# Where the 1/rms of a gated group norm is applied: before the branch product, or on its group sums

## The chip, the cores and the metric

The kernel runs on one core of one Trainium2 chip. The metric is device time in microseconds (us) of one launch. Engines: PE (TensorE, matrix products; PEld is its weight load), DVE (VectorE), ACT (ScalarE), POOL (GpSimd, which does not read the matrix accumulators), SP (SyncE, which here only issues DMAs). PSUM is the accumulator memory that PE writes, one bank of it holds 128x512 float32; SBUF is the working memory.

## The reference, cut to what matters

One encoder layer for 256 rows (tokens) of width 1024. The part that the change touches is the end of the SSD branch and the merge:

```python
y_ssd = y_ssd + d_skip[:, None] * xh                       # 256 x 2048
y_ssd = gated_group_rmsnorm(y_ssd, z, ssd_norm)
merged = sigmoid(gate_a) * (y_attn @ w_attn_branch) + sigmoid(gate_b) * (y_ssd @ w_ssd_branch)
x = x + merged @ w_out
x = x + hier_moe(rmsnorm(x))                               # 32 experts, float32 weights

def gated_group_rmsnorm(y, z, g):                          # 4 groups of 512 columns
    yf = y * silu(z)
    yg = yf.reshape(..., 4, 512)
    yg = yg * rsqrt(mean(yg * yg, -1) + EPS)
    return yg.reshape(yf.shape) * g
```

The factor rsqrt(...) is one number for each row and group. The product with w_ssd_branch sums over the columns of all four groups.

## The kernel before, in words

Every float32 operand of the large products is split in two float32r parts, hi and lo (a tile `..._hl`, or yT, mT, hT with a hi and a lo plane), and a product takes three passes: hi·hi, hi·lo, lo·hi. Weights come from memory as `w_raw` (four buffers, SP issues their DMAs in order), ACT casts hi, and DVE or POOL subtracts to get lo. A weight chunk of 512 columns is eight row blocks k of 128 rows, 48 matmuls for its two row tiles t, and its hi and lo go through six buffers that PE must free again. Chunks stand in one list, `wsrc`; `next_w` hands out the next and loads one ahead.

Stages in order: input projections and attention (to about 185 us of the trace), four SSD groups of 512 columns (products xs and z, scans), two chunks A (attention branch product), four chunks S (SSD branch product), the output product o, routing, and the experts. 100 MB of expert weights, tiles `we`, are fetched by `prefetch` calls that stand between the stages; each waits in SP's queue for a buffer that the stage before has freed. From the routing on, PE works through eight sets q of four experts, each with 12 MB of weights.

SSD, group g: `ssd_y(g, q)` makes yg (two 128x256 tiles of columns by rows, so columns lie on partitions), squares it on ACT, and POOL adds the squares into ysum. `ssd_tail(g)` (called later, ahead of others by its priority) sums over the partitions with a matmul by ones (ps_n, L769), forms 1/rms for each row (DVE nv L771, POOL power L100), and, since rows lie on the free dimension of yg, spreads it over the partitions with a product by the identity (ps_r, L775). Then DVE multiplies yg by the gain snorm and ps_r (L781, four times 128x256), ACT casts hi (L783), DVE subtracts lo (L784) into yT[g].

Branch product S, row halves i of w_ssd_branch outside, column halves c inside: `wide_chunk("S", yT[2i:2i+2])` sums two groups into one PSUM tile for each t. DVE multiplies it by (tab_b + 1), where tab holds the tanh of the gates (L832). For i = 0 POOL adds it to the attention part in tab (L834). For i = 1 DVE adds (L836), PE transposes (ps_mT L839), ACT and DVE split into mT, and a `prefetch` follows.

The order on each engine is set by a scheduler with its own timeline, under the priorities in the code; it can move any instruction if others change.

Of the kernel before, what the change touches and what calls it, by code (L numbers as in the profile page):

```python
# [11 lines left out]
F32 = mybir.dt.float32  # L12
# [3 lines left out]
AF = mybir.ActivationFunctionType  # L16
ALU = mybir.AluOpType
# [31 lines left out]
def block_kernel(ctx, tc, xin, idn, ngain, catt, cprep, cssd, cmoe, cwr, wsm, wwide, win, wgu, wdn, out, dbg=None):  # L49
    nc = tc.nc  # L50
    pe, act, dve, pool = nc.tensor, nc.scalar, nc.vector, nc.gpsimd

    cst = ctx.enter_context(tc.tile_pool(name="cst", bufs=1))
# [629 lines left out]
    snorm = C("snorm")  # L683
    yT = [bigt([P, 2, 4, T], F32R, f"yT{g}") for g in range(4)]
# [22 lines left out]
    st_ = {}  # L707
# [30 lines left out]
    def ssd_y(g, q):  # L738
# [3 lines left out]
        st_[g, q, "yg"] = yg  # L742
# [3 lines left out]
        for h2 in range(2):  # L746
# [9 lines left out]
            dve.tensor_tensor(yg[:, h2, :], yg[:, h2, :], zs[:, h2, :], op=ALU.mult)  # L756
        sq = zs_t[g, q]
# [7 lines left out]
    def ssd_tail(g):  # L765
# [4 lines left out]
        r = ssd.tile([P, 2], F32, tag="nv", name="nv")  # L770
        dve.tensor_scalar(r, ps_n, 1.0 / 512, 4 * EPS, op0=ALU.mult, op1=ALU.add)  # L771
        power(r, r, None)
        ps_r = paux.tile([P, T], F32, tag="n", bufs=1, name="ps_r")
        for t in range(2):
            pe.matmul(ps_r[:, t * P:(t + 1) * P], lhsT=r[:, t:t + 1].to_broadcast([P, P]), rhs=ident,  # L775
                      start=True, stop=True)
        for q in range(2):
            yg = st_[g, q, "yg"]
            for b in range(2):
                ct = 4 * g + 2 * q + b  # L780
                dve.scalar_tensor_tensor(yg[:, b, :], yg[:, b, :], snorm[:, ct:ct + 1], ps_r, op0=ALU.mult, op1=ALU.mult)  # L781
            hl = yT[g][:, :, 2 * q:2 * q + 2]
            act.copy(hl[:, 0], yg)  # L783
            dve.tensor_sub(hl[:, 1], yg, hl[:, 0].bitcast(F32))  # L784
# [441 lines left out]
def prep(inp):  # L1226
# [26 lines left out]
    wide += [wa[:, :, o] for o in halves] + [ws[:, 8 * i:8 * i + 8, o] for i in range(2) for o in halves]  # L1253
# [57 lines left out]
```

## Time and profile before

| | |
|---|---|
| median of 3 runs | 583.99 us (583.7 to 587.01) |
| profiled execution, its own time | 585.1 us |
| its span, first to last instruction | 583.3 us |
| PE, DVE, ACT, POOL busy, share of the span | 95%, 57%, 47%, 41% |
| mean granted PE clock | 0.987 of full |
| bytes read | 157.5 MB, mean 272 GB/s |

The profile is one execution: 1.8 us of its time lie outside the span. Busy time of PE counts modelled ends of overlapped matmuls, so what counts is when matmuls start, and the pace between starts.

### The profile page before, as it was taken

The numbers are of one execution on the slowest core, as the hardware profiler recorded it, in microseconds if no ns is written. First come the engines' busy times: TensorE is split into PE (matmuls) and PEld (weight loads), VectorE is DVE, ScalarE is ACT, GpSimd is POOL, SyncE is SP. The second block draws the span as 40 slices with busy tenths as digits, with TensorE's granted clock in tenths as the row PEclk, the third lists the DMA queues.
The fourth block names the chain that finished last, engine by engine and source line by source line (L and its number), as shares of the span: only waits on it lengthen the run. The fifth ranks groups of instructions, "written<-read, shape, count | busy, mean of one in ns | idle before, by whom it ended". The sixth has DMA issues, their size and how long they took to land.

```text
span 583.3 us, 9898 instructions
## 1 busy us (share of the span) xinstructions
PE 552.6 (95%) x3605; PEld 400.6 (69%) x3605; DVE 330.9 (57%) x689; ACT 271.8 (47%) x633; POOL 239.5 (41%) x254
## 2 busy tenths in 40 slices
PE   8999989999999999999999999999998898988976
PEld 5878768798898999898878888964453452433512
DVE  3659975999996778989695657451111121111101
ACT  7567557757987877878764436410000000000001
POOL 4687584775844456656567745210000000000000
PEclk9999999999999999999999999999989997999989
DMA  7755244453435488645568589989999999999993
GB/s 272 250 162 169 103 147 146 144 174 124 128 122 186 149 323 334 217 149 185 208 194 300 177 307 389 405 344 417 419 417 408 420 417 421 409 415 421 420 407 123
DMA packets 35123, 159.27 MB, mean 273 GB/s; under 512 B 4096, under 2 KB 5760, under 8 KB 25856
## 3 DMA queue, kind: packets, MB, share of 16 engines
q1 hardware_dynamic: 33776, 157.30, 71.8%
q10 hardware_dynamic: 1296, 1.30, 0.7%
q8 instruction: 30, 0.49, 0.3%
q14 instruction: 21, 0.17, 0.1%
HBM read 157.54 MB, written 1.05 MB: 272 GB/s over the span
## 4 chain that ended last, share of the span: by engine, by line
PE 69%; DMA 12%; DVE 9%; issue 4%; POOL 3%; ACT 3%; SPq 0%; ACTq 0%; POOLq 0%; DVEq 0%
PE ps_S L294 8%; PE pgu L1037 6%; PE ps_xs L241 6%; PE ps_g L294 6%; DMA we<-wdn 5%; DMA we<-wgu 5%; PE ps_z L241 5%; PE py L1097 4%; PE ps_A L294 4%; PE acc L1112 4%; PE ps_g L1030 4%; PE ps_q L294 3%; PE ps_o L241 2%; PE ps_o L294 2%; PE ps_iq L294 2%
## 5 line engine op out<-in xcount | busy, mean ns | idle before, releaser
L156 POOL TENSOR_TENSOR w_hl<-w_raw,w_hl 128x512 fp32r<-128x512 f32 (+1 forms) x101 | 141.6, 1406 | 81.8 <-ACT w_hl L152 66.5
L152 ACT CAST w_hl<-w_raw 128x512 fp32r<-128x512 f32 (+1 forms) x212 | 125.7, 620 | 46.4 <-PE ps_S L294 18.5
L156 DVE TENSOR_TENSOR w_hl<-w_raw,w_hl 128x512 fp32r<-128x512 f32 (+1 forms) x111 | 100.4, 911 | 38.7 <-ACT w_hl L152 38.1
L1055 POOL TENSOR_TENSOR dc<-Dm,cmr 128x128 f32<-128x128 f32 x16 | 6.1, 401 | 143.5 <-DVE Dm L960 137.4
L1037 PE MATMUL pgu<-we,xg 128*32 128x512 f32 x512 | 60.2, 603 | 3.9 <-DMA we<-wgu 3.9
L241 PE MATMUL ps_z<-hT,w_hl 128*128 128x256 f32 x384 | 51.7, 286 | 0.0
L241 PE MATMUL ps_xs<-hT,w_hl 128*128 128x256 f32 x384 | 50.7, 285 | 0.0
L241 PEld LDWEIGHTS ps_z<-hT,w_hl 128*128 128x128 f32 x384 | 47.8, 190 | 2.0 <-issue 2.0
L241 PEld LDWEIGHTS ps_xs<-hT,w_hl 128*128 128x128 f32 x384 | 47.6, 191 | 2.1 <-issue 2.1
L294 PE MATMUL ps_g<-w_hl,gT 128*128 128x512 f32 x192 | 48.1, 399 | 0.0
L294 PE MATMUL ps_S<-w_hl,yT 128*128 128x512 f32 x192 | 44.6, 391 | 0.0
L1033 DVE TENSOR_TENSOR xg<-ps_g,cmoe 128x512 f32<-128x512 f32 (+2 forms) x18 | 11.3, 631 | 57.4 <-PE ps_g L1030 57.4
L1030 PEld LDWEIGHTS ps_g<-Dm,x_sb 128*128 128x128 f32 x256 | 31.0, 191 | 14.9 <-issue 9.7
L294 PEld LDWEIGHTS ps_g<-w_hl,gT 128*128 128x128 f32 x192 | 34.9, 188 | 9.3 <-DVE w_hl L156 1.0
L294 PEld LDWEIGHTS ps_S<-w_hl,yT 128*128 128x128 f32 x192 | 35.8, 188 | 7.4
L1037 PEld LDWEIGHTS pgu<-we,xg 128*32 128x32 f32 x512 | 15.1, 110 | 37.1 <-issue 26.1
L1097 PE MATMUL py<-we,aTt 128*32 128x512 f32 (+1 forms) x272 | 35.8, 616 | 3.8 <-DVE aTt L1083 2.1
L1108 ACT COPY y<-py 128x512 f32<-128x512 f32 (+1 forms) x9 | 4.8, 539 | 66.9 <-PE py L1097 66.9
L1075 DVE SCALAR_TENSOR_TENSOR ac<-th,pgu 128x256 f32<-128x256 f32 x8 | 3.4, 421 | 57.5 <-ACT th L1073 57.5
L1112 PE MATMUL acc<-y,dcT 128*128 128x512 f32 (+1 forms) x68 | 32.6, 606 | 0.9 <-DVE y L1110 0.8
L1030 PE MATMUL ps_g<-Dm,x_sb 128*128 128x128 f32 x256 | 33.4, 280 | 0.0
L1073 ACT ACTIVATE th<-pgu,rs 128x256 f32<-128x256 f32 x8 | 3.8, 474 | 55.1 <-PE pgu L1037 55.1
(296 smaller groups left out, 968.9 us busy)
## 6 DMA issues: line engine op xcount, KB each, us to landing
we<-wgu SPq DMA_DIRECT2D x55, 1024.0 KB, 13.8
w_raw<-wwide SPq DMA_DIRECT2D x60, 512.0 KB, 3.9
w_raw<-win SPq DMA_DIRECT2D x44, 512.0 KB, 3.9
we<-wdn SPq DMA_DIRECT2D x17, 1024.0 KB, 17.4
we<-wdn SPq DMA_DIRECT2D x28, 512.0 KB, 12.0
we<-wgu SPq DMA_DIRECT2D x18, 512.0 KB, 10.2
x_sb<-xin SPq DMA_DIRECT2D x2, 512.0 KB, 4.4
we<-wdn SPq DMA_DIRECT2D x4, 256.0 KB, 11.5
```

Of the source, the lines that this page charges most:

```text
L152: return act.copy(self.hl[i][:, 0], self.raw[i])
L156: return eng.tensor_sub(hl[:, 1], self.raw[i], hl[:, 0].bitcast(F32))
L241: pe.matmul(ps, lhsT=lhs[k][:, a], rhs=rhs[k][:, b], start=j == 0 and k == 0 and i == 0, stop=j == len(regions) - 1 and k == KD - 1 and i ...
L294: pe.matmul(ps[t], lhsT=lhs[t][k][:, a], rhs=w[k][:, b], start=k == 0 and i == 0, stop=k == KD - 1 and i == 2)
L1030: pe.matmul(ps[:, kk, :], lhsT=x1[:, t, (k + kk) * P:(k + kk + 1) * P], rhs=Dm[:, t].rearrange("p e j -> p (e j)"), start=t == 0, stop=t == 1)
L1033: dve.tensor_tensor(xg[:, ks, :], ps, fgain[:, ks].unsqueeze(2).to_broadcast([P, n, P]), op=ALU.mult)
L1037: i = pe.matmul(pgu[32 * e:32 * e + 32, :], lhsT=xg[:, k, 32 * e:32 * e + 32], rhs=wg[k][e], start=k == 0, stop=k == KD - 1, tile_position ...
L1055: pool.tensor_tensor(dc[:, t], Dm[:, t], cmr[:, t, 4 * q:4 * q + 4].unsqueeze(2).to_broadcast([P, 4, NSLOT]), op=ALU.mult)
L1073: act.activation(th, pgu[:, 0:256], AF.Tanh, scale=rs)
L1097: i_py = pe.matmul(py[32 * e:32 * e + 32, :], lhsT=aTt[:, f, 32 * e:32 * e + 32], rhs=wd[2 * n + f][e][:, c], start=f == 0, stop=f == 1, t ...
L1108: act.copy(y, py)
L1112: pe.matmul(acc[t][n][:, c], lhsT=dcT[:, t * P:(t + 1) * P], rhs=y, start=False, stop=q == 7 and c.stop == 512)
```

## The change

The gain snorm stays with yg, and 1/rms is left out of yT. `ssd_y` now splits yg at once: ACT writes hi = yg * snorm, DVE writes lo = yg * snorm - hi, each in two pieces of 128x256. `ssd_tail` keeps only ps_n and the power, into one tile rg for all groups; ps_r, the four multiplications, the casts and the subtractions of the tail are gone. In the S stage each group has a PSUM sum of its own, rows on partitions, so 1/rms is a scalar for each partition: the first group's sum goes through ACT with that scale into a tile m, the next two are multiplied by rg and added on DVE, and after two groups more the gate is applied. tab_b gets its + 1 once, on ACT. Column halves are now outside, row halves inside, and the list of weights follows (`ws[...] for o in halves for i in range(2)`).

```diff
+    rg = cst.tile([P, 4, 2], F32, name="rg")
...
+        hl = yT[g][:, :, 2 * q:2 * q + 2]
+        for b in range(2):
+            ct = 4 * g + 2 * q + b
+            act.activation(hl[:, 0, b], yg[:, b], AF.Copy, scale=snorm[:, ct:ct + 1])
+            dve.scalar_tensor_tensor(hl[:, 1, b], yg[:, b], snorm[:, ct:ct + 1], hl[:, 0, b].bitcast(F32),
+                                     op0=ALU.mult, op1=ALU.subtract)
...
-        r = ssd.tile([P, 2], F32, tag="nv", name="nv")
+        r = rg[:, g]
         dve.tensor_scalar(r, ps_n, 1.0 / 512, 4 * EPS, op0=ALU.mult, op1=ALU.add)
         power(r, r, None)
-        ps_r = paux.tile([P, T], F32, tag="n", bufs=1, name="ps_r")
-        for t in range(2):
-            pe.matmul(ps_r[:, t * P:(t + 1) * P], lhsT=r[:, t:t + 1].to_broadcast([P, P]), rhs=ident, ...)
-        for q in range(2):
-            yg = st_[g, q, "yg"]
-            for b in range(2):
-                ct = 4 * g + 2 * q + b
-                dve.scalar_tensor_tensor(yg[:, b, :], yg[:, b, :], snorm[:, ct:ct + 1], ps_r, ...)
-            hl = yT[g][:, :, 2 * q:2 * q + 2]
-            act.copy(hl[:, 0], yg)
-            dve.tensor_sub(hl[:, 1], yg, hl[:, 0].bitcast(F32))
...
-    for i in range(2):
-        for c in range(2):
-            ps = wide_chunk("S", yT[2 * i:2 * i + 2], LAG)
+    for c in range(2):
+        for t in range(2):
+            act.activation(tab[t, c][:, 1], tab[t, c][:, 1], AF.Copy, bias=1.0)
+        U = [mo2.tile([P, 512], F32, tag="y", name="mg") for _ in range(2)]
+        for i in range(2):
...
+                    if kk % 4 == 0:
+                        pss[t, g] = (pacc.tile([P, 512], F32, tag=f"acc{t}1", name="ps_S") if g
+                                     else pmm.tile([P, 512], F32, tag="mm", name="ps_S"))
...
+            for g, t in ((0, 0), (0, 1), (1, 0), (1, 1)):
                 ta, tb = tab[t, c][:, 0], tab[t, c][:, 1]
-                m = mo2.tile([P, 512], F32, tag="y", name="mg")
-                dve.scalar_tensor_tensor(m, tb, 1.0, ps[t], op0=ALU.add, op1=ALU.mult)
-                if i == 0:
-                    pool.tensor_add(ta, m, ta)
+                ps, m, r1 = pss[t, g], U[t], rg[:, 2 * i + g, t:t + 1]
+                if 2 * i + g == 0:
+                    act.activation(m, ps, AF.Copy, scale=r1)
+                elif 2 * i + g < 3:
+                    dve.scalar_tensor_tensor(m, ps, r1, m, op0=ALU.mult, op1=ALU.add)
+                    if i:
+                        dve.tensor_mul(m, m, tb)
+                        pool.tensor_add(ta, m, ta)
+                if 2 * i + g < 3:
                     continue
+                dve.scalar_tensor_tensor(m, ps, r1, tb, op0=ALU.mult, op1=ALU.mult)
                 dve.tensor_add(m, m, ta)
```

PE, around the tail of group 0, before (ps_z is the product for z of group 2, py the scan products, ps_b a spread of decays):

```order
L241 MATMUL ps_z_3087<-hT_209,w_hl 128x256 x10
L749 MATMUL py<-e_2902,xdt_2895 64x256
L775 MATMUL ps_r<-ident,nv 128x128 x2
L749 MATMUL py<-e_2902,xdt_2895 64x256
L752 MATMUL py<-e_2902,xdt_2895 64x128 x2
L749 MATMUL py<-e_2903,xdt_2895 64x256
L729 MATMUL ps_b<-acsT,iir 128x256
L749 MATMUL py<-e_2903,xdt_2895 64x256
L752 MATMUL py<-e_2903,xdt_2895 64x128 x2
L241 MATMUL ps_z_3087<-hT_209,w_hl 128x256 x14
```

The same place now:

```order
L241 MATMUL ps_z_3088<-hT_209,w_hl 128x256 x13
L749 MATMUL py<-e_2911,xdt_2904 64x256 x2
L241 MATMUL ps_z_3088<-hT_209,w_hl 128x256 x7
L752 MATMUL py<-e_2911,xdt_2904 64x128 x2
L730 MATMUL ps_b<-acsT,iir 128x256
L241 MATMUL ps_z_3088<-hT_209,w_hl 128x256
L749 MATMUL py<-e_2912,xdt_2904 64x256 x2
L752 MATMUL py<-e_2912,xdt_2904 64x128 x2
L241 MATMUL ps_z_3088<-hT_209,w_hl 128x256 x3
```

ps_r is gone, and matmuls of the z product now stand between the scan products.

DVE, end of the first pass over S, before (`trs` is a small table for the routing):

```order
L832 SCALAR_TENSOR_TENSOR mg<-tab,ps_S 128x512 x2
L156 TENSOR_TENSOR w_hl<-w_raw,w_hl 128x512 x4
L832 SCALAR_TENSOR_TENSOR mg<-tab,ps_S 128x512 x2
L836 TENSOR_TENSOR mg<-mg,tab 128x512 x2
L156 TENSOR_TENSOR w_hl<-w_raw,w_hl 128x512 x2
```

The end of the first column half now:

```order
L156 TENSOR_TENSOR w_hl<-w_raw,w_hl 128x512 x3
L848 SCALAR_TENSOR_TENSOR mg<-ps_S,rg,mg 128x512 x2
L850 TENSOR_TENSOR mg<-mg,tab 128x512 x2
L156 TENSOR_TENSOR w_hl<-w_raw,w_hl 128x512
L854 SCALAR_TENSOR_TENSOR mg<-ps_S,rg,tab 128x512
L855 TENSOR_TENSOR mg<-mg,tab 128x512
L854 SCALAR_TENSOR_TENSOR mg<-ps_S,rg,tab 128x512
L156 TENSOR_TENSOR w_hl<-w_raw,w_hl 128x512
L855 TENSOR_TENSOR mg<-mg,tab 128x512
L156 TENSOR_TENSOR w_hl<-w_raw,w_hl 128x512 x2
```

Eight instructions on sums stand where four stood, and splits of the next weights stand behind and between them.

SP, the stretch with the weights of S and the expert tiles we_11 and we_0, before:

```order
L270 DMA we_10_3942<-wdn 128x2048
L141 DMA w_raw<-wwide 128x1024 x10
L270 DMA we_11_4261<-wdn 128x2048
L270 DMA we_0_4263<-wgu 128x2048
L141 DMA w_raw<-wwide 128x1024 x4
```

And now:

```order
L270 DMA we_10_3939<-wdn 128x2048
L141 DMA w_raw<-wwide 128x1024 x7
L270 DMA we_11_4168<-wdn 128x2048
L270 DMA we_0_4170<-wgu 128x2048
L141 DMA w_raw<-wwide 128x1024 x8
```

The two expert tiles now go out one weight chunk earlier, ahead of the last chunk of S.

## Rows read from the trace of the kernel before

**Rows 1.** The page: busy time by engine.

```profile
PE 552.6 (95%) x3605; PEld 400.6 (69%) x3605; DVE 330.9 (57%) x689; ACT 271.8 (47%) x633; POOL 239.5 (41%) x254
```

**Rows 2.** The chain that ended last, near its end: start us, us, what.

```profile
541.82 19.88 DMA we<-wgu
561.74 1.94 PE pgu L1037 x8
```

**Rows 3.** Windows: PE, PEld, DVE, ACT, POOL busy, PE clock, DMA share, GB/s.

```profile
185.00:308.00 123.00, 122.84 (x915) 108.28 (x912) 106.14 (x190) 92.75 (x204) 72.46 (x61) 1.00 0.63 221
...
308.00:353.00 45.00, 45.00 (x208) 37.41 (x207) 26.20 (x38) 20.58 (x36) 28.13 (x23) 1.00 0.78 263
...
388.00:390.00 2.00, 2.00 (x17) 1.04 (x17) 0.75 (x3) 0.00 (x0) 0.76 (x2) 1.00 0.32 127
...
400.00:560.00 160.00, 143.25 (x1006) 64.09 (x1004) 25.88 (x60) 9.55 (x20) 4.55 (x12) 0.97 1.02 417
```

**Rows 4.** SP's waits from 376 to 410: us in total, times, longest.

```profile
SPq L270 <- PE pgu L1037: 13.3, 7, 8.2
```

**Rows 5.** Timeline of PE around the ps_r of each group: start us, us.

```profile
212.07 0.65 PE L749 MATMUL py<-e,xdt 128*64 128x256 f32 x4
...
212.88 1.33 PE L241 MATMUL ps_z<-hT,w_hl 128*128 128x256 f32 x9
...
235.70 0.65 PE L749 MATMUL py<-e,xdt 128*64 128x256 f32 x2
...
238.82 1.34 PE L241 MATMUL ps_z<-hT,w_hl 128*128 128x256 f32 x9
...
261.59 0.61 PE L775 MATMUL ps_r<-ident,nv 128*128 128x128 f32 x4
262.04 0.27 PE L716 MATMUL ps_x<-ident,xs 128*128 128x128 f32 x1
...
292.23 0.65 PE L749 MATMUL py<-e,xdt 128*64 128x256 f32 x4
...
293.82 0.38 PE L729 MATMUL ps_b<-acsT,iir 128*128 128x256 f32 x1
...
321.78 0.61 PE L775 MATMUL ps_r<-ident,nv 128*128 128x128 f32 x4
322.14 25.90 PE L294 MATMUL ps_S<-w_hl,yT 128*128 128x512 f32 x113
```

**Rows 6.** Groups of instructions, 184 to 360 us: count, busy us, mean ns, idle before.

```profile
L606 DVE SCALAR_TENSOR_TENSOR xs<-xs,acc 128x256 f32<-128x256 f32 x12 | 7.8, 666 | 0.0
L784 DVE TENSOR_TENSOR yT<-yg,yT 128x512 fp32r<-128x512 f32 x8 | 7.8, 974 | 0.3 <-ACT yT L783 0.3
...
L834 POOL TENSOR_TENSOR tab<-mg,tab 128x512 f32<-128x512 f32 x4 | 5.6, 1400 | 1.8 <-DVE mg L832 1.8
...
L832 DVE SCALAR_TENSOR_TENSOR mg<-tab,ps_S 128x512 f32<-128x512 f32 x8 | 5.3, 678 | 1.7 <-PE ps_S L294 1.7
L783 ACT CAST yT<-yg 128x512 fp32r<-128x512 f32 x8 | 5.1, 637 | 0.9 <-DVE yg L781 0.9
...
L605 ACT ACTIVATE xs<-acc 128x256 f32<-128x256 f32 x12 | 4.8, 416 | 3.1 <-DVE acc L603 3.1
L836 DVE TENSOR_TENSOR mg<-mg,tab 128x512 f32<-128x512 f32 x4 | 3.9, 1008 | 0.0
```

**Rows 7.** The tile yg: ns min/median/max of its DVE instructions.

```profile
L756 DVE TENSOR_TENSOR yg<-yg,zs x16: 410/465/1308, 213.6 to 309.8; 128x256 f32<-128x256 f32 x16
L781 DVE SCALAR_TENSOR_TENSOR yg<-yg,cssd,ps_r x16: 462/475/480, 237.0 to 323.6; 128x256 f32<-128x256 f32 x16
```

**Rows 8.** Groups 307 to 360 us: weight splits on DVE and ACT in the S stage.

```profile
L152 ACT CAST w_hl<-w_raw 128x512 fp32r<-128x512 f32 x35 | 21.5, 623 | 25.5 <-PE ps_S L294 18.5 <-DMA w_raw<-wwide 3.2 <-issue 1.9
L156 DVE TENSOR_TENSOR w_hl<-w_raw,w_hl 128x512 fp32r<-128x512 f32 x18 | 15.9, 889 | 15.6 <-ACT w_hl L152 15.5
```

**Rows 9.** SP's timeline: issue of the expert tiles in S.

```profile
337.84 1.24 SPq L270 DMA_DIRECT2D we<-wdn  x1
```

More of the change, by code (lines that the diff above doesn't have):

```diff
@@ L824, in block_kernel @@
     pacc = ctx.enter_context(tc.tile_pool(name="pacc", bufs=1, space=PSUM, reuse_waits="tile"))
-    for i in range(2):
-        for c in range(2):
-            ps = wide_chunk("S", yT[2 * i:2 * i + 2], LAG)
-            for t in range(2):
-                ta, tb = tab[t, c][:, 0], tab[t, c][:, 1]
-                m = mo2.tile([P, 512], F32, tag="y", name="mg")
-                dve.scalar_tensor_tensor(m, tb, 1.0, ps[t], op0=ALU.add, op1=ALU.mult)
-                if i == 0:
-                    pool.tensor_add(ta, m, ta)
+    for c in range(2):
[3 more added lines that the diff above has]
+        for i in range(2):
+            w = pairs(next_w(), slice(0, 512))
+            src = pairs(yT[2 * i:2 * i + 2], slice(0, T))
+            pss = {}
+            for k in range(KD + LAG):
+                for t in range(2):
+                    kk = k - LAG * t
+                    if not 0 <= kk < KD:
+                        continue
+                    g = kk // 4
+                    if kk % 4 == 0:
+                        pss[t, g] = (pacc.tile([P, 512], F32, tag=f"acc{t}1", name="ps_S") if g
+                                     else pmm.tile([P, 512], F32, tag="mm", name="ps_S"))
+                    for a, b in PASSES:
+                        pe.matmul(pss[t, g], lhsT=src[kk][:, a, t * P:(t + 1) * P], rhs=w[kk][:, b],
+                                  start=kk % 4 == 0 and (a, b) == PASSES[0], stop=kk % 4 == 3 and (a, b) == PASSES[2])
+            for g, t in ((0, 0), (0, 1), (1, 0), (1, 1)):
+                ta, tb = tab[t, c][:, 0], tab[t, c][:, 1]
+                ps, m, r1 = pss[t, g], U[t], rg[:, 2 * i + g, t:t + 1]
[7 more added lines that the diff above has]
+                if 2 * i + g < 3:
                     continue
+                dve.scalar_tensor_tensor(m, ps, r1, tb, op0=ALU.mult, op1=ALU.mult)
                 dve.tensor_add(m, m, ta)
@@ L1252, in prep @@
     halves = [slice(0, 512), slice(512, 1024)]
-    wide += [wa[:, :, o] for o in halves] + [ws[:, 8 * i:8 * i + 8, o] for i in range(2) for o in halves]
+    wide += [wa[:, :, o] for o in halves] + [ws[:, 8 * i:8 * i + 8, o] for o in halves for i in range(2)]
     wwide = np.stack(wide + [wo[:, :, 0:512]])
```

4 lines of the change are left out of this document (removed).

## The prediction

> **What bounds the kernel now.** I read the busy shares first, then the chain from its end, then the windows, and last PE's timeline, stage by stage. PE is busy 95% of the span and DVE 57% [rows 1], but the average hides two programs. The chain ends in expert weights: a transfer of 19.88 us until 561.7, with PE's last expert products right behind it [rows 2], and from 400 to 560 the DMA engines are full, at 417 GB/s [rows 3]. So the end is set by when that stream begins to flow without a break. The window 388 to 390 answers that: there DMA falls to a share of 0.32 [rows 3], because every free buffer is filled and SP waits, 8.2 us at the longest, for PE's first expert products (pgu) to free one [rows 4]. From then on the stream never stops. The end is therefore the time at which PE reaches pgu, plus a constant. PE gets there through stages in which it starts matmuls almost without gaps: 113 matmuls of S in 25.9 us, 0.229 us each [rows 5]. What counts for this change is whatever makes PE arrive at about 388 earlier or later, one for one. DVE, ACT and POOL count only where PE waits for them.
>
> **The change, part by part.**
>
> *ps_r leaves PE.* An undisturbed py block (half of a head group) takes 0.81 us, 212.07 to 212.88. In group 0 the two py blocks around ps_r, with one small ps_b, take 3.12 us (235.70 to 238.82), where two blocks alone take 1.62: 1.50. Group 1: 0.45 (261.59 to 262.04). Group 2: a py block with ps_r inside takes 1.59 (292.23 to 293.82) less 0.81: 0.78. Group 3: 0.36 (321.78 to 322.14) [all rows 5]. Sum 3.1; I take **-3.0** for the ps_b in the first. The bounds are 4 x 0.36 = 1.4, if the rest of those waits has other causes and stays, and 3.1.
>
> *DVE and ACT in the SSD stage.* Removed: 16 multiplications at 0.475 [rows 7] and 8 subtractions at 0.974 [rows 6], 15.4 us of DVE; and 8 casts at 0.637, 5.1 of ACT. Added: 16 lo pieces of 128x256 with two SBUF inputs. The nearest row is L606, the same operation and shape, 0.666: 10.7 us. And 16 hi pieces on ACT, nearest L605, 0.416: 6.7 us [rows 6]. DVE gains 4.7 us, ACT loses 1.6 over 140 us. DVE is busy 106 of 123 us here, ACT 93 [rows 3], so neither sets PE's pace by volume; zero on PE, with the waits already counted at ps_r. If that cover were gone, it would show as DVE gain, so zero is the cautious side.
>
> The new lo pieces read two SBUF tensors; the multiplications that they replace read PSUM for one. The rows tell these apart: with PSUM 462 to 480 ns, with two SBUF inputs 410 at best and 1308 at worst [rows 7]. The Trainium skill (SBUF — State Buffer, Who interferes with whom) says why, and it speaks against this change: a DVE instruction with two SBUF inputs contends with a GpSimd one that reads SBUF, and the later of the two blocks fully. The trace agrees with the spread; by the rule taken at its worst the change would come out slower, the third rival below.
>
> *+ 1 on tab.* Four ACT instructions of 128x512, nearest L783, 0.637: 2.5 us, which the order puts at about 100 to 130 us, in the attention. Something waits behind each on ACT (casts of weights, the move of qT). ACT is not that stage's limit; I put **+0.3** on PE, between 0 and 2.5.
>
> *The S stage.* PE's 192 matmuls stay. The sums of one group instead of two: 16 instead of 8. Four go to ACT (0.637 each by L783, 2.5 us), 12 to DVE at 0.678 where 8 were: +2.7; four multiplications by tab_b, nearest L836, 1.008: +4.0; the additions on POOL and DVE stay four and four [rows 6]. DVE goes from 26.2 busy in 45 us [rows 3] to some 29, since the group 3 tail (four L781 and two L784, 3.8 us) leaves the window. Volume is no problem: ACT's casts of weights wait 18.5 us for PE here [rows 8], so splits run ahead as far as six buffers allow. The order is the problem. At the end of each column half DVE has to take the last sums before the next splits: 0.678 + 1.008 + 0.678 + a split of 0.889 [rows 6, 8] = 3.3 us after the last group of the first row tile, and an addition of 1.400 on POOL has to be done before. PE has work that needs no new split for about 11 matmuls there, 2.5 us at 0.229. So each of the two ends costs 0 to 0.8 us, or up to 2.2 if the POOL addition is late by its whole length. The ps_n of group 3 now stands after 24 matmuls of S, where 36 stood, and behind ACT's two new hi pieces. I take **+1.3** for all these, between 0 and 5.
>
> *Expert prefetch.* Two tiles of 1 MB went out at 337.84 and after [rows 9], when the third S chunk's code was through; now they follow the second chunk, some 11 us earlier (48 x 0.229). From 308 to 353 DMA has 22% free, 9.9 us [rows 3], and 2 MB take 5.0 us at 417 GB/s. It fits. It lengthens the dry spell at 388 and brings nothing there, since PE's arrival still decides; it does make sure that the stream does not come after PE. Zero. SP passes four more weight loads behind these two tiles; the four raw buffers are waited for anyway.
>
> **Sum:** -3.0 + 0.3 + 1.3 = -1.4 us on the profiled execution: span 583.3 to 581.9, its own time 585.1 to 583.7. The median of the runs is 1.1 below that execution: 583.99 - 1.4 = **582.6 us**.
>
> **Rivals.**
>
> 1. *S takes its sums for free.* The order may place the splits well enough that PE never waits in S, and yg, free of the tail, may remove other small waits in the SSD stage. For it: ACT and DVE were idle about half the S stage [rows 8]. Against: the splits stand behind the sums in DVE's order. Then -3.0 to -4.5: 579.5 to 581.
>
> 2. *DVE's in-order queue makes PE wait at the ends of the halves* (the other side). Place: the sums of groups 2 and 3, with POOL's additions among weight splits of 1.4 us each. It decides as soon as the chain there is over 2.5 us by more than the 3.0 that ps_r gives back, spread over two ends and the start of S, that is from 1.5 us at each end on. At 2.2 for each end and 2 for ps_n of group 3 and the first order change of chunks: +6.4 - 3.0 = +3.4, 587.4; at the threshold 584. For it: eight DVE instructions in the place of four. Against: 45 us with 26 busy.
>
> 3. *The shared reads of DVE and POOL.* If each of the 14 lo pieces before 308 us were blocked for a whole POOL operation (0.410 + 1.400 = 1.8 us), DVE's 106.1 would become 106.1 - 5.7 - 5.8 + 25.3 = 119.9 of 123; with the idle of before (17 us) kept, the stage would last 137: +14 - 3 = +11, 595. The mean of L606 at 0.666, in the same mix of POOL work, speaks against all of it.
>
> 4. *Nothing arrives at the end.* If the stream had been ready later than PE, PE's gain would be lost and the time stay at 584.0. Against it is the dry window at 388.
>
> **How the numbers follow.** Forecast (582.6, its own range 581 to 584) 0.55; rival 1 0.17; rival 2 0.18; rival 3 0.02; rival 4 0.08. Of each of the tails about a tenth is left out: the range reaches from rival 1's far end, 579.5, to inside rival 2, 586.5. One per cent, about what a measurement of this kernel can tell from no change, is 5.8 us. Faster by that needs more than twice all that ps_r costs: 0.06. Slower by that needs rival 3, or rival 2 well past its price: 0.06. The rest, 0.88, is within.
>
> **What would show it.** Right: two py blocks near 236 with their ends about 1.5 us sooner; S beginning 2 to 3 us earlier than 307.6; 192 matmuls of S within 45 to 47 us; the dry DMA window now 3 us or more long and ending one to two us earlier than 391; then the same 417 GB/s. Rival 2 would show PE idle, or PE's weight load waiting for w_hl from DVE or POOL, just after the last matmul of a half. Rival 3 would show lo pieces of over 1 us in the mean. I am wrong altogether if the stretch before 185 us, where only the order moves, shifts by more than 1.5 us, or if the stream breaks off again after 392.

## The result and the profile after

| | before | after |
|---|---|---|
| median of 17 runs each | 583.99 us | 587.69 us (585.76 to 590.53) |
| ratio after to before, 95% interval | | 1.0067 [1.0055, 1.0079] |
| profiled execution, its own time | 585.1 us | 587.59 us |
| its span | 583.3 us | 585.7 us |

Slower by 3.7 us, where 1.4 us less was forecast. The page's busy line of the changed kernel and the end of its chain answer to [rows 1, 2]:

```profile
PE 550.4 (94%) x3589; PEld 398.1 (68%) x3589; DVE 342.5 (58%) x689; ACT 276.8 (47%) x649; POOL 246.0 (42%) x254
...
544.53 19.89 DMA we<-wgu
564.47 1.93 PE pgu L1056 x8
```

PE has 16 matmuls less (ps_r) and is busy 2.2 us less, yet the last expert products start 2.7 us later (561.74 before). DVE, which was to have 4.7 us less work in SSD and 6.7 more in S, is 11.6 busier. The windows (columns as in [rows 3]):

```profile
185.00:308.00 123.00, 122.32 (x903) 107.03 (x899) 109.44 (x186) 94.59 (x211) 73.17 (x62) 1.00 0.62 218
308.00:353.00 45.00, 44.13 (x203) 36.18 (x200) 34.05 (x44) 22.94 (x42) 30.55 (x23) 1.00 0.80 273
...
390.00:394.00 4.00, 4.00 (x33) 2.08 (x33) 0.74 (x3) 0.00 (x0) 0.76 (x2) 1.00 0.64 230
400.00:560.00 160.00, 142.65 (x1008) 63.90 (x1000) 26.45 (x61) 10.03 (x21) 4.56 (x12) 0.98 1.02 417
```

The stream of experts is the same (417 GB/s), and there is a dry spell ahead of it as before, only 2 us later. So 2.0 of the 2.7 us lie ahead of 390 (first expert product 388.26 before, 390.25 after); the other 0.7 are taken up below the table. PE's timeline of the changed kernel at the borders of its stages (start us, us, what, and in brackets PE's wait and who ended it; L840 is S, L294 and L241 are the 512- and the 256-column chunks of o, L886 the warm-up products of the routing):

```profile
151.61 1.96 PE L241 MATMUL ps_xs<-hT,w_hl 128*128 128x256 f32 x15
...
308.12 4.84 PE L840 MATMUL ps_S<-w_hl,yT 128*128 128x512 f32 x20
313.84 0.61 PE L776 MATMUL ps_n<-ones,ysum 128*128 128x1 f32 x4 [0.87 <-POOL ysum L768]
314.31 21.36 PE L840 MATMUL ps_S<-w_hl,yT 128*128 128x512 f32 x93
...
353.45 4.70 PE L294 MATMUL ps_o<-w_hl,mT 128*128 128x512 f32 x20
...
359.35 0.60 PE L858 MATMUL ps_mT<-ident,mg 128*128 128x128 f32 x4
360.73 0.39 PE L241 MATMUL ps_o<-w_hl,mT 128*128 128x256 f32 x1 [0.78 <-ACT w_hl L152]
...
384.49 2.54 PE L886 MATMUL ps_w<-on 128*128 128x512 bf16 x11
...
390.25 1.06 PE L1056 MATMUL pgu<-we,xg 128*32 128x512 f32 x8
```

The same borders before (L769 is ps_n):

```profile
315.83 0.50 PE L769 MATMUL ps_n<-ones,ysum 128*128 128x1 f32 x4
...
353.07 5.83 PE L294 MATMUL ps_o<-w_hl,mT 128*128 128x512 f32 x24
...
382.51 2.54 PE L867 MATMUL ps_w<-on 128*128 128x512 bf16 x11
...
388.26 1.07 PE L1037 MATMUL pgu<-we,xg 128*32 128x512 f32 x8
```

Two gaps are new: ahead of ps_n of group 3 and at the start of o. To compare kernels, PE's way is cut by these starts: from the first x product (which came at 150.5 to 152.2 us in all profiles, the same kernel included, so it is the zero here) to the first o matmul, from there to the warm-up products, to the first expert product, and to the last one. Before's first entry, for example, is 353.07 - 152.15. In the three kernels marked * one matmul of o stands among the last of S; there the border is the start of the other o matmuls less 0.23.

| kernel | SSD and S | o | warm-up | to last pgu | ratio to before, 95% |
|---|---|---|---|---|---|
| before | 200.92 | 29.44 | 5.75 | 173.48 | |
| after | 201.84 | 31.04 | 5.76 | 174.22 | 1.0067 [1.0055, 1.0079] |
| order_alone * | 200.92 | 32.37 | 5.75 | 174.10 | 1.0079 [1.0047, 1.0110] |
| order_alone_mT_first * | 200.92 | 29.23 | 5.75 | 174.04 | 1.0016 [1.0001, 1.0031] |
| order_prefetch_late * | 200.93 | 31.28 | 8.20 | 173.87 | 1.0036 [1.0018, 1.0055] |
| before_prefetch_early | 200.92 | 29.87 | 5.79 | 173.40 | 1.0067 [1.0043, 1.0090] |
| prefetch_late | 201.90 | 32.34 | 5.75 | 174.55 | 1.0100 [1.0077, 1.0124] |
| sums_in_pmm | 200.89 | 31.28 | 5.75 | 173.23 | 1.0030 [1.0012, 1.0047] |
| pmm_weights_first | 200.84 | 31.06 | 5.77 | 174.55 | 1.0037 [1.0023, 1.0052] |
| pmm_mT_first | 200.87 | 29.35 | 5.75 | 174.81 | 1.0004 [0.9989, 1.0019] |
| pmm_mT_zs_first | 199.98 | 29.32 | 5.75 | 174.99 | 0.9994 [0.9979, 1.0009] |
| old_order_pmm | 200.83 | 32.03 | 8.02 | 173.00 | 1.0054 [1.0034, 1.0074] |
| ps_r_twice | 204.13 | 29.21 | 5.75 | 174.34 | 1.0078 [1.0062, 1.0094] |

In after, 0.9 us are lost up to o and 1.6 in o. A second profile of the changed kernel (after_look, below) gave 201.86, 30.80, 5.75 and 173.90: the first three repeat within 0.3 us. They need not: three profiles of before_prefetch_early (experiment 3) took 200.92, 202.07 and 200.94 up to o, so a difference of 1 us in one profile counts here only where the wait that makes it is seen in the trace. The last column scatters by 2 us with no relation to the edits, and is largest where PE comes early. It is read as the stream's own scatter, not as a cause; no experiment tested that.

### The profile page after: what moved, and what is told of

Its sections match the earlier page's. It is cut to its first block, busy times and chain, and to the rows that moved or that the text cites. A ratio compares the mean times of both kernels' runs of the same rounds, so it can differ in the third digit from the quotient of the medians.

```text
span 585.7 us, 9882 instructions
## 1 busy us (share of the span) xinstructions
PE 550.4 (94%) x3589; PEld 398.1 (68%) x3589; DVE 342.5 (58%) x689; ACT 276.8 (47%) x649; POOL 246.0 (42%) x254
## 4 chain that ended last, share of the span: by engine, by line
PE 55%; DVE 18%; DMA 13%; ACT 6%; issue 5%; POOL 3%; ACTq 0%; SPq 0%; DVEq 0%; POOLq 0%
PE pgu L1056 6%; PE ps_S L840 6%; DMA we<-wdn 5%; DMA we<-wgu 5%; DVE w_hl L156 4%; PE py L1116 4%; PE ps_xs L241 4%; PE ps_g L1049 4%; PE acc L1131 4%; PE ps_z L241 3%; PE ps_q L294 2%; PE ps_g L294 2%; PE ps_o L241 2%; DVE acc L603 2%; PE ps_iq L294 2%
## 5 line engine op out<-in xcount | busy, mean ns | idle before, releaser
L156 POOL TENSOR_TENSOR w_hl<-w_raw,w_hl 128x512 fp32r<-128x512 f32 (+1 forms) x101 | 145.3, 1445 | 78.4 <-ACT w_hl L152 63.1
L156 DVE TENSOR_TENSOR w_hl<-w_raw,w_hl 128x512 fp32r<-128x512 f32 (+1 forms) x111 | 106.0, 963 | 25.4 <-ACT w_hl L152 24.9
L241 PE MATMUL ps_z<-hT,w_hl 128*128 128x256 f32 x384 | 51.9, 286 | 0.0
L241 PE MATMUL ps_xs<-hT,w_hl 128*128 128x256 f32 x384 | 50.6, 285 | 0.6 <-DVE zs L703 0.6
L241 PEld LDWEIGHTS ps_z<-hT,w_hl 128*128 128x128 f32 x384 | 47.8, 190 | 2.6 <-issue 2.2
L241 PEld LDWEIGHTS ps_xs<-hT,w_hl 128*128 128x128 f32 x384 | 47.5, 191 | 2.9 <-issue 2.1
L294 PE MATMUL ps_g<-w_hl,gT 128*128 128x512 f32 x192 | 47.8, 398 | 0.0
L840 PE MATMUL ps_S<-w_hl,yT 128*128 128x512 f32 x192 | 45.1, 392 | 0.0
L1049 PEld LDWEIGHTS ps_g<-Dm,x_sb 128*128 128x128 f32 x256 | 31.3, 191 | 15.5 <-issue 11.1
L294 PEld LDWEIGHTS ps_g<-w_hl,gT 128*128 128x128 f32 x192 | 35.1, 188 | 8.8 <-DVE ss_q L333 0.8
L840 PEld LDWEIGHTS ps_S<-w_hl,yT 128*128 128x128 f32 x192 | 35.7, 188 | 7.8 <-DVE w_hl L156 0.4
L1131 PE MATMUL acc<-y,dcT 128*128 128x512 f32 (+1 forms) x68 | 30.7, 576 | 0.1
```

The source lines that it names most:

```text
L156: return eng.tensor_sub(hl[:, 1], self.raw[i], hl[:, 0].bitcast(F32))
L241: pe.matmul(ps, lhsT=lhs[k][:, a], rhs=rhs[k][:, b], start=j == 0 and k == 0 and i == 0, stop=j == len(regions) - 1 and k == KD - 1 and i ...
L294: pe.matmul(ps[t], lhsT=lhs[t][k][:, a], rhs=w[k][:, b], start=k == 0 and i == 0, stop=k == KD - 1 and i == 2)
L840: pe.matmul(pss[t, g], lhsT=src[kk][:, a, t * P:(t + 1) * P], rhs=w[kk][:, b], start=kk % 4 == 0 and (a, b) == PASSES[0], stop=kk % 4 == 3 ...
L1049: pe.matmul(ps[:, kk, :], lhsT=x1[:, t, (k + kk) * P:(k + kk + 1) * P], rhs=Dm[:, t].rearrange("p e j -> p (e j)"), start=t == 0, stop=t == 1)
L1131: pe.matmul(acc[t][n][:, c], lhsT=dcT[:, t * P:(t + 1) * P], rhs=y, start=False, stop=q == 7 and c.stop == 512)
```

## The experiments

**1. The order of the halves alone.** The kernel before, with

```diff
-    for i in range(2):
-        for c in range(2):
+    for c in range(2):
+        for i in range(2):
             ps = wide_chunk("S", yT[2 * i:2 * i + 2], LAG)
```

and the list of weights to match; the prefetch after `i == 1` so comes after the second weight chunk.

> The kernel before with one thing changed: column halves outside and row halves inside in S, with the weight list and the expert prefetch behind them; sums, 1/rms and splits as before. Theory: the changed kernel loses in four places, at ps_n of group 3 (about 1.1 us of PE waiting, from the PSUM of the group sums), in the o stage (1.6 us, from the order that an early prefetch gives), in the stream after 398 us (about 0.5), and in the SSD stage, where nothing was gained. Only the middle two can be here: 584.5 to 586. Rival A, the order of the halves is the whole loss: 587 to 588. Rival B, the order of the halves costs nothing: 583.5 to 584.5.

588.65 us, 4.0 more than the kernel before in the same runs: rival A, and beyond it. The SSD and S stages are those of before to 0.01 us, and o takes 2.9 us more. ACT's and PE's timelines at the start of o show how:

```profile
359.64 1.14 ACT L152 CAST w_hl<-w_raw 128x512 fp32r<-128x512 f32 x2 [2.48 <-DMA w_raw<-win]
360.69 0.64 ACT L844 CAST mT<-ps_mT 128x256 fp32r<-128x256 f32 x2
```

```profile
357.65 1.03 PE L839 MATMUL ps_mT<-ident,mg 128*128 128x128 f32 x8
360.31 0.38 PE L241 MATMUL ps_o<-w_hl,mT 128*128 128x256 f32 x1 [1.63 <-ACT w_hl L152]
361.04 1.21 PE L241 MATMUL ps_o<-w_hl,mT 128*128 128x256 f32 x8 [0.34 <-DVE w_hl L156]
```

ACT's next instruction is the cast of the first 256-column weights of o, and they land at 359.6. The casts of mT, whose whole input is there from 358.7 on, stand behind it. PE's next instruction is a matmul on the same weights, so both engines wait for one DMA while 24 matmuls of the 512-column chunk could run (experiment 2 has them at 358.71). In the kernel before, ACT had the first casts of mT ahead:

```profile
359.38 0.81 ACT L844 CAST mT<-ps_mT 128x256 fp32r<-128x256 f32 x2 [1.14 <-PE ps_mT L839]
360.53 1.14 ACT L152 CAST w_hl<-w_raw 128x512 fp32r<-128x512 f32 x2 [0.34 <-DMA w_raw<-win]
```

**2. The casts of mT ahead.** order_alone, with the splits of that chunk (number 36) behind the last cast of mT, which `last_mT` keeps:

```diff
+                if n == 36:
+                    st.enter_context(tc.issue_after(last_mT[0].ins))
                 wready[n].split(KSP_FEW if n in FEW else KSP)
```

> order_alone (kernel before with column halves outside) with one thing more: the splits of the first 256-column chunk of o are issued behind the last cast of mT, so ACT cannot stand waiting for those weights (2.48 us at 357.2 to 359.6 in order_alone) while the casts of mT queue behind it. Theory: the order on ACT and PE at the start of the o stage is what order_alone loses: PE's wait of 1.63 and 0.34 us goes, o comes back from 32.4 to 30 us or less, the time from 588.6 to 585.5 to 586.5. Rival: the weights are late for PE in any order, and the wait moves to the place where the 256-column matmuls now begin: 587.5 to 589.

585.10 us, 0.9 more than before in the same runs, o in 29.23. The same places:

```profile
358.29 1.68 ACT L847 CAST mT<-ps_mT 128x256 fp32r<-128x256 f32 x4 [1.12 <-PE ps_mT L842]
359.86 1.14 ACT L152 CAST w_hl<-w_raw 128x512 fp32r<-128x512 f32 x2
```

```profile
357.65 1.03 PE L842 MATMUL ps_mT<-ident,mg 128*128 128x128 f32 x8
358.71 5.72 PE L297 MATMUL ps_o<-w_hl,mT 128*128 128x512 f32 x24
```

The theory holds: the sequence of a few instructions on ACT and PE was worth 3 us, and the work is the same.

**3. What puts the order wrong: halves or prefetch?** Three kernels move the prefetch of the first two expert tiles alone, `if i: prefetch(...)` to `if c: prefetch(...)` with the loops as they stand: in order_alone back to the third chunk (order_prefetch_late), in the kernel before on to the second (before_prefetch_early), in the changed kernel back (prefetch_late).

> order_alone with the first two expert tiles of S issued after the third weight chunk again, so that only the order of the halves is left. Theory: the early tiles let the scheduler count on the o weights too soon; with the tiles late, ACT's casts of mT stand ahead again and half or more of the 4 us comes back: 584.5 to 586. Rival: it is the order of the halves that makes the o stage late, whatever the tiles do: 587.5 to 589.

587.10 us: half of the loss comes back, and neither side is right alone. At o's start the waits are nearly gone, but o still takes 31.3 us; the profile has the granted clock at half from 382 on, so its last part and its 8.20 us of warm-up (below, the last section) are no measure of the edit.

> The kernel before with one thing changed: the first two expert tiles of S are issued after the second weight chunk, as in the changed kernel, with the order of the halves as before. The prediction put this at zero. Theory: it is not zero, since it moves the o weights and the casts in the scheduler's order: 585.5 to 588. Rival, the prediction: 583.5 to 584.8.

588.62 us, so the prediction's zero for the prefetch is wrong, but the profile shows 29.87 in o and no more. Its own time, 585.5, was the fastest of seven, so two more profiles were taken:

> before_prefetch_early once more, for a second profile. Its profile showed 0.5 us more than the kernel before up to the first expert product, and the fastest of its times, 585.5; its median was 588.6. Theory: in most executions the granted clock falls to half near 382 us, in the routing, as in the profiles of old_order_pmm and order_prefetch_late, where the stretch from the last warm-up products to the first expert product took 8.0 and 8.2 us in place of 5.75: with 588 us the profile shows that. Rival: the stream of expert weights is what is longer by 3 us, with the clock full until 424.

> The same again, for a third profile: a half clock near 382 us with 587 us and more, none with 586 us and less (theory); a longer stream (rival).

586.55 and 584.16 us. Up to o they took 202.07 and 200.94, then 29.87 in o and 5.79 in the warm-up both; to the last pgu 173.75 and 173.30. The clock was full until 424 us or later in both, and the stream was not longer. The rival is not seen; the theory speaks of executions of 587 us and more, and neither was one, so it stays untested. In the first, PE waited for late weights inside S (0.35 and 0.20 us above its pace near 342 and 344 the longest, POOL's split named once), 1.1 us in all. Why most runs took 588 stays open. The mean granted clock on record is 0.982 to 0.983 in the five runs from 587.66 us on and 0.985 and 0.988 in the two below, so the longer ones had more half clock somewhere; a mean does not say where.

> The changed kernel with the first two expert tiles of S issued after the code of the third weight chunk again, as before the change, in place of the second. Theory: PE's order in the o stage then takes the wide product before the first matmul of the 256-column one, the wait of 0.78 us for its weights at 360 us goes, and about 1 to 1.6 us come back: 586.1 to 586.7. Rival: the o stage is late because the last sums of S are late (the chain of DVE behind the last matmul), so the wait only gets another name: 587.4 to 588.

590.31 us: the wait took another name, and grew. PE's timeline:

```profile
359.75 0.63 PE L858 MATMUL ps_mT<-ident,mg 128*128 128x128 f32 x4 [0.91 <-DVE mg L855]
...
361.68 1.20 PE L294 MATMUL ps_o<-w_hl,mT 128*128 128x512 f32 x4 [0.84 <-DVE mT L864]
```

The 512-column chunk now comes first on PE, as expected, but ACT's two casts of the o weights still stand ahead of three casts of mT, and DVE's last sums end 1.2 us later than in after. So late tiles alone do not cure the changed kernel: the order around the start of o decides, and each edit deals it anew. What early tiles cost by themselves stays open with the 588.62 above.

**4. Where the group sums lie.** The changed kernel, its first S chunk with all four sums in the three buffers of the wide products:

```diff
-                        pss[t, g] = (pacc.tile([P, 512], F32, tag=f"acc{t}1", name="ps_S") if g
+                        pss[t, g] = (pacc.tile([P, 512], F32, tag=f"acc{t}1", name="ps_S") if g and c + i
                                      else pmm.tile([P, 512], F32, tag="mm", name="ps_S"))
```

> The changed kernel with all four group sums of the first S chunk in the three PSUM buffers that wide products use, not two of them in the memory that the SSD stage's small PSUM tiles held. Theory: group 1's sums need no longer wait for that memory, so ps_n of group 3 can stand behind 31 matmuls of S in place of 24, and PE's gap at 312.6 to 313.8 us closes: -1.1 us, 586.6. Rival: the squares of group 3 are what is late, PE waits there for them anyway or for a PSUM buffer instead: 587.4 to 588.

586.38 us, SSD and S 0.95 us shorter. PE's timeline, to be read against 313.84 above:

```profile
308.36 6.44 PE L840 MATMUL ps_S<-w_hl,yT 128*128 128x512 f32 x27
314.63 0.51 PE L776 MATMUL ps_n<-ones,ysum 128*128 128x1 f32 x4
315.00 3.35 PE L840 MATMUL ps_S<-w_hl,yT 128*128 128x512 f32 x13
```

The pool `pacc` lies over the five PSUM banks of the SSD stage's small tiles, ps_n among them, and is opened when that stage closes. With group 1's sums in it, no matmul of group 1 came ahead of ps_n, whose squares were not ready: in the changed kernel ACT did the last hi piece ahead of the square, and POOL the sum after that, until 313.8 (ACT, then POOL):

```profile
310.74 0.51 ACT L761 ACTIVATE yT<-yg,cssd 128x256 fp32r<-128x256 f32 x1 [1.93 <-DVE yg L756]
311.16 0.61 ACT L765 ACTIVATE zs<-yg 128x512 f32<-128x512 f32 x1
```

```profile
312.73 1.06 POOL L768 TENSOR_TENSOR ysum<-ysum,zs 128x256 f32<-128x256 f32 x1
```

Before, ps_n stood behind 36 matmuls of S, at 315.83, and waited for nothing. The Trainium skill (Perfetto Trace Analysis, Matmul Optimizations) asks to use all eight PSUM banks. Here the kernel with fewer banks in this place was the faster one, 1.0030 against 1.0067: the banks were not free, they still belonged to a stage whose last product was late. (The wait is for that place in PE's order and not for the bank's reader: the first S matmul behind ps_n starts at 314.31, and DVE reads ps_n at 314.49.)

**5. The o weights ahead of the expert tiles.** sums_in_pmm with `prefetch(PF1[2] + PF1[3])` behind the call that loads the first 256-column weights.

> sums_in_pmm with the first 256-column weights of o issued ahead of the last two expert tiles of the S stage, in place of behind them. Theory: those weights stand behind 2 MB of expert tiles on the DMA engines and so land at 359.5 us; ahead of them they land some 3 to 5 us sooner, ACT does not wait (3.03 us in sums_in_pmm) and PE's wait of 1.02 us at 360 goes: 585 to 585.5 against 586.4, and no loss in the stream, since the tiles are only waited for after 390. Rival: what ends the wait is mT, which the last sums set, and it stays: 586 to 587.

586.31 us: the rival's time, by another way. The first weights landed early enough for ACT, and PE's wait there fell to 0.26; but the second 256-column chunk now stood behind four expert tiles, and PE waited for that:

```profile
359.25 1.58 PE L241 MATMUL ps_o<-w_hl,mT 128*128 128x256 f32 x11 [0.26 <-DVE w_hl L156]
...
372.36 0.51 PE L241 MATMUL ps_o<-w_hl,mT 128*128 128x256 f32 x2 [1.24 <-ACT w_hl L152]
```

**6. Both cures on the changed kernel.** The edits of 2 and 4 together.

> The changed kernel with both cures: the first chunk's sums in the PSUM of the wide products, and the splits of the first 256-column chunk of o behind the last cast of mT. Theory: PSUM at ps_n and the order at the start of o are the loss of the change, and the SSD stage is level with before, so it comes back to the kernel before: o in 29.4 us in place of 31.3, 584 to 585. Rival: a third loss is left, the DVE chain behind the last sums of S (two more instructions, 1.4 to 1.8 us each in the trace), and o still takes 30.5 us or more: 585.5 to 586.5.

584.25 us, ratio 1.0004 [0.9989, 1.0019]: the whole loss is recovered. Up to the first expert product PE needs 200.87 + 29.35 + 5.75 = 235.97 us, before 236.11. The rival's third loss is not there: at the start of o PE waits 0.3 us.

**7. The group sums with the old order of halves.** `for i, c in ((0, 0), (0, 1), (1, 0), (1, 1))` around the changed sums (each row half gated by itself, so POOL adds eight times), prefetch and weight list as before, with the edit of 4.

> The group sums of the changed kernel (no ps_r, 1/rms on the sums, hi and lo at once), but row halves outside and column halves inside as before, with the expert prefetch where it was, and the first chunk's sums in the PSUM of the wide products. The sums of each row half are scaled and gated by themselves, so POOL adds eight times in place of four. Theory: the halves' order and PSUM carry the whole loss, so this comes out level with the kernel before or a little under: 583 to 585. Rival: the group sums themselves lose (eight more instructions on sums behind each half): 586 or more.

587.67 us: the rival. PE waits 1.18 us at 360 for the second mT, behind DVE's last addition (1.76 us, where the like took 1.008 in [rows 6]) and two splits among the sums. So this form of the group sums, with four more additions on POOL, also loses without the new order. The cure of experiment 2 was not tried on it, and how much of the 3.2 us is the half clock in some runs (its profile has it at 382.8) was not separated.

**8. The price of ps_r.** The kernel before with the two matmuls of ps_r done twice, `for t in (0, 1, 0, 1)`.

> The kernel before with the product that spreads 1/rms (ps_r) done twice over, into the same PSUM tile: eight more matmuls of 128x128, the rest as before. It measures the term of the prediction. Theory: ps_r costs PE what its own four matmuls take, 0.36 us for each group, so twice is 1.1 to 1.4 us more than the kernel before, +0.2% (and the scheduler moves other matmuls into the place, so it may be less). Rival, the prediction's term: 0.75 for each group with the waits around it, +3.0 us, +0.5%.

588.89 us. SSD and S took 3.2 us more, the size of the prediction's term and over the theory's 1.4. But the places do not bear the term out. Counted from the start of each of PE's matmuls to the start of the next, ps_r holds 2.09 us before and 3.52 here: 1.4 more, the theory's price. The z products hold 0.96 more and S 1.20 more, where the schedule is another: PE waits 0.31 and 0.13 us at 274 and 276 for DVE's decays (tile e), for example. That these add up to the term's 3 us is luck as far as it can be seen.

**9. Without the lo pieces.** Two kernels take the lo pieces' load away. lo_one_input: `dve.tensor_scalar(hl[:, 1, b], yg[:, b], snorm, 2.0 ** -13, mult, mult)` (shortened) in the changed kernel, so lo holds other numbers. no_lo: pmm_mT_first without the 16 instructions, S reading hi in their place; it leaves the lo part of that product out.

> The changed kernel with the lo pieces written by a DVE instruction that reads yg alone (yg times the gain times a small constant, in place of minus hi), so the lo half of yT holds other numbers: the products have the same size, the results do not. Theory: the lo pieces, which read two tiles of SBUF, make DVE's and POOL's other work longer (the weight splits on DVE took 1048 ns in the mean from 184 to 360 us, 917 before) and so keep the SSD stage from gaining: the splits should come back to 900 to 960 ns, and the time to 585.7 to 586.7. Rival: the SSD stage gains nothing because ps_r cost PE no more than its own four times 0.36 us, and DVE's length is hidden: the splits get shorter, the time stays at 587.2 to 588.2.

> pmm_mT_first with the lo pieces left out: S reads the hi half in place of lo in its third pass, so PE does as many matmuls as ever, and the results are those of a product without that part. It leaves out 16 DVE instructions of 0.746 us in the SSD stage. Theory: ps_r's removal gave back some 1.4 us, and the lo pieces in DVE's queue took it again (PE waits 0.73 us at 224 for DVE's zs, and 0.3 twice more); without them the SSD stage is 1 to 1.5 us shorter than in pmm_mT_first, 155.6 to 154.4. Rival: the waits are where other work stands, ps_r was covered, and the SSD stage stays at 155.4 to 155.8.

595.97 and 589.90 us, both slower, and both undecided. With another cost for these instructions the scheduler dealt the whole stage anew: in lo_one_input the last scan product came at 314.4, 6.6 us later than in after, PE waited 2.2 us for ps_n of group 3, and the granted clock was half from 319 to 326; in no_lo PE stood 2.5 us ahead of ps_n of group 3 (to 317.9). The splits on DVE did get shorter (948 and 912 ns from 184 to 308 us, 991 in after), as the theory had it, and it bought nothing. An edit that changes an instruction's cost can't isolate it in this kernel.

**10. One instruction moved.** pmm_mT_first, with yg * zs (first half of the second unit) behind zs of the next product on DVE:

```diff
+                if q and g < 3 and not h2:
+                    st.enter_context(tc.issue_after(zev[0].ins))
                 dve.tensor_tensor(yg[:, h2, :], yg[:, h2, :], zs[:, h2, :], op=ALU.mult)
```

> pmm_mT_first with one instruction in each of three groups put behind another on DVE: the multiplication of yg by zs waits in order until zs of the next group's z product is written, so the z sums leave PSUM first. DVE, ACT, PE and POOL do the same work. Theory: PE's wait of 0.73 us at 223 (its x product waits for a PSUM buffer that DVE's zs frees, behind a multiplication of 1.51 us) is the part of ps_r's gain that DVE's queue took back, and it goes: 583.3 to 584, the SSD stage at 154.9. Rival: PE waits there for something else of the same time, or the delayed multiplication makes py's reader late: 584.2 to 585.

DVE in pmm_mT_first, and then here:

```profile
221.00 1.51 DVE L759 TENSOR_TENSOR yg<-yg,zs 128x256 f32<-128x256 f32 x1
222.43 0.41 DVE L706 SCALAR_TENSOR_TENSOR zs<-zs,ps_z 128x256 f32<-128x256 f32 x1
```

```profile
220.73 0.41 DVE L707 SCALAR_TENSOR_TENSOR zs<-zs,ps_z 128x256 f32<-128x256 f32 x1
221.06 1.18 DVE L763 TENSOR_TENSOR yg<-yg,zs 128x256 f32<-128x256 f32 x1
```

The 1.51 us began beside a split on POOL and ended 0.29 us after it (the last section has the count):

```profile
220.48 1.74 POOL L156 TENSOR_TENSOR w_hl<-w_raw,w_hl 128x512 fp32r<-128x512 f32 x1
```

The kernel before had zs first too (221.65, yg * zs 221.99). PE's wait at 223 (0.73 us above its pace, 0.57 of it idle) is gone, and SSD and S take 199.98, 0.9 less than in the kernel before. Not all of the 0.9 is this wait: from start to start, z holds 0.70 more than in pmm_mT_first and A 0.55 less, so other places were dealt anew too. The time is 583.43 us against 583.43 of the kernel before in the same runs: 0.9994 [0.9979, 1.0009], no faster than a measurement can tell. As a version to keep it is level with before.

**11. How far a profile repeats.**

> The changed kernel once more, for a second profile. Theory: its times of 585.8 to 590.5 are the same program with or without the half clock near 382 us; PE's stretches up to 382 are as in the first profile within 0.1 us. Rival: the stretches themselves vary by 1 us or more from one execution to the next, and the comparison of stretches of single profiles proves little.

587.94 us; the stretches differ by 0.02, 0.24 and 0.01 us, without a half clock near 382 in either profile. That is over the theory's 0.1 in o and far under the rival's 1 us, though the rival has its case in experiment 3. The mean granted clock of the 17 runs falls as their time grows (0.987 at 585.8 and 585.9 us, 0.981 at 590.1 and 590.5); that the spread comes from a half clock near 382 is not shown.

## Why the prediction was wrong

Two steps failed. In the profiles, up to the last pgu, -1.4 us was forecast and +2.7 came. SSD and S were to win 1.7 (-3.0 + 1.3) and lost 0.9; o was to stay and lost 1.6; the stream behind is 0.7 longer, within its scatter; and the first x product came 0.5 us sooner, where 0.3 later was forecast. The larger step is "ps_r leaves PE", -3.0, with "zero on PE" for DVE's new work: none of it arrived. The other is "Expert prefetch ... Zero".

**"Expert prefetch ... Zero", and with it the sentence that S's ends are the place where the order costs.** The new order was priced inside S alone. Inside S the ends of the halves cost nothing: 93 matmuls stand dense behind ps_n, at 0.23 us. What the order of halves and tiles changed is the next stage: which of two casts stands first on ACT when a DMA is late. order_alone has none of the group sums and is 4.0 us behind before; order_alone_mT_first is 0.9 behind, and the 3.1 between them are o's. In the changed kernel the same cure took o from 31.28 (sums_in_pmm) to 29.35 (pmm_mT_first). The prediction had the DMA queue in view ("SP passes four more weight loads") and counted bytes, which fit; it did not ask who stands behind the load on ACT.

**ps_r leaves PE, -3.0.** It did not arrive: with the PSUM wait cured, SSD and S took 200.89, before 200.92. The term was also too large: from start to start ps_r held 2.09 us of PE before, and the py pieces around it, which the term counted in, hold 13.53 before and 13.48 after. The same count over pmm_mT_first, which has SSD and S as long as before, shows where the 2.09 went: ps_x holds 1.14 more (0.73 is the wait at 223 behind it, which experiment 10 took away), S 0.54, ps_b 0.42 (behind two of them, at 231 and 261, the z product starts 0.20 and 0.30 us late) and z 0.20. What put each of these there was tested for the wait at 223 alone; the kernels of experiment 9 could not do it.

**DVE and ACT in SSD, zero.** The new instructions were priced a little low: lo pieces 746 ns (estimate 666), hi 508 (416). What was left out is what they do to the others. Groups from 184 to 360 us (columns as in [rows 6]), first after, then before:

```profile
L156 DVE TENSOR_TENSOR w_hl<-w_raw,w_hl 128x512 fp32r<-128x512 f32 x49 | 51.1, 1048 | 8.2 <-ACT w_hl L152 7.9
...
L756 DVE TENSOR_TENSOR yg<-yg,zs 128x256 f32<-128x256 f32 x16 | 12.1, 755 | 0.2
L762 DVE SCALAR_TENSOR_TENSOR yT<-yg,cssd,yT 128x256 fp32r<-128x256 f32 x16 | 11.9, 746 | 2.2 <-ACT yT L761 2.2
...
L606 DVE SCALAR_TENSOR_TENSOR xs<-xs,acc 128x256 f32<-128x256 f32 x12 | 9.5, 805 | 0.1
...
L735 DVE TENSOR_TENSOR e<-e,cb 128x512 f32<-128x512 f32 x16 | 13.3, 829 | 2.4 <-ACT e L734 2.4
```

```profile
L156 DVE TENSOR_TENSOR w_hl<-w_raw,w_hl 128x512 fp32r<-128x512 f32 x49 | 44.8, 917 | 22.8 <-ACT w_hl L152 22.4
...
L734 DVE TENSOR_TENSOR e<-e,cb 128x512 f32<-128x512 f32 x16 | 15.2, 955 | 1.3 <-ACT e L733 1.2
...
L756 DVE TENSOR_TENSOR yg<-yg,zs 128x256 f32<-128x256 f32 x16 | 10.1, 632 | 0.2
```

The splits, yg * zs and xs (666 before, [rows 6]) take 6.3 + 2.0 + 1.7 = 10 us more for work that did not change; e * cb takes 2.0 less. All of them read two tiles of SBUF, and each is long just when it begins beside a running POOL instruction; the last section has the count. The Trainium skill (SBUF — State Buffer, Who interferes with whom) says that issue order, not the operation's shape, decides who blocks, and the trace agrees: in the kernel before they took 0.50 us more behind POOL, else 0.01. So rival 3 had the mechanism, with the wrong payer: it put the price on the new instructions alone, at most 14 times, and it fell on whatever began behind POOL, on nine of the 16 lo pieces among others. Its 595 did not come: DVE's idle time ahead of the splits took it up, 22.8 us before and 8.2 after.

**+ 1 on tab, +0.3.** The start of the stage differs by as much between profiles of kernels that are the same up to there (150.5 to 152.2), so this term was not resolved.

**The S stage, +1.3.** Of this term one part was found: 0.95 us at ps_n, the PSUM wait. That is rival 2's "ps_n of group 3", priced at up to 2; its other half, the ends of the halves, was not there. So rival 2 named the right side, 584 to 587.4, and one of its two places; that its far end came so near to 587.69 is luck, since 1.6 us of the loss lie in o, which it left out.

**PE's arrival plus a constant.** Over 17 profiles (all but lo_one_input) the last pgu moves by 0.88 us for each us of the first, with a scatter of 0.5. It held: the slope's error is 0.08, so one for one is not excluded. The scatter makes gains of under 1 us hard to see at the end.

The signs that were named: py blocks near 236 did not end sooner (238.82 before, 239.79 after, with eight more z matmuls done); S began 1.7 us earlier, but with two py pieces still to do, so at 308.12 PE had done four S matmuls, and before two: some 0.5 us ahead, all of it from ahead of 152 us, where profiles differ anyway.

## What to carry to other kernels

Price a change of order at the next stage border too: list for each in-order engine what stands behind the first instruction that waits for a DMA, and ask what would run if the DMA were 2 us late. When new tiles go into a PSUM pool that lies over a closing stage's pool, the last product of the old stage can become a wait of the new one. Before adding DVE work, look at what POOL runs beside it: the price can fall on old instructions. Where a scheduler deals the order, hold one instruction behind another to test a cause; changing an instruction's cost tests the scheduler instead.

## What the runs showed of the hardware

**Two inputs in SBUF beside POOL.** From 184 to 360 us the kernel before has 105 DVE instructions in six groups that read two tiles of SBUF (L156, L606, L734, L756, L784, L836). 53 of them began while a POOL instruction had 60 ns or more to run. They took 0.50 us more than the shortest of their kind in the mean, and 50 of the 53 ended 0.28 us (128x256) or 0.55 us (128x512) after POOL's instruction did. The other 52 took 0.01 us more in the mean. After, it is 68 of 117, 0.57 us more, 66 ending so, and 0.01 for the other 49: 39 us of such extra time, where it was 26. The 16 instructions with one of their two inputs in PSUM (L755) took 465 to 482 ns before, though nine began beside POOL.

**The half clock.** In two profiles (order_prefetch_late, old_order_pmm) the granted clock fell to half for some 7 us in the middle of the routing, at the second of two waits of PE for xT (0.35 and 0.46 us), and the warm-up products there took 4.89 us where 2.54 is usual. lo_one_input had such drops too, the first in S, from 319 us on. Windows of order_prefetch_late (columns as in [rows 3]), and the warm-up in PE's timeline:

```profile
382.00:384.00 2.00, 2.00 (x10) 1.65 (x10) 1.00 (x7) 0.00 (x0) 0.00 (x0) 0.50 1.05 424
384.00:386.00 2.00, 2.00 (x6) 0.70 (x5) 1.92 (x19) 0.00 (x0) 0.00 (x0) 0.50 1.00 399
386.00:388.00 2.00, 2.00 (x6) 0.66 (x5) 0.11 (x1) 0.00 (x0) 0.00 (x0) 0.50 0.95 381
```

```profile
383.36 4.89 PE L867 MATMUL ps_w<-on 128*128 128x512 bf16 x11
```

That is 1.2 GHz where the work wants 2.4, 2.3 to 2.5 us on the path, and more than most edits here are worth. The kernel before had its half clocks only from 424 us on, where PE waits for the stream in any case (1.44 us ahead of the products at 559.25, 1.43 ahead of the last). After shows no such drop and has the same kind of waits on xT (0.45 and 0.46), so the waits alone do not bring it about; what does was not found.
